# Seven-product pairs whose sums stay in two PSUM banks, in pairs 3 to 21 of the last three feed-forwards

## The chip, the core and the metric

One core of a Trainium2 chip runs the whole program in one launch. TensorE (PE) multiplies, VectorE (DVE), ScalarE (ACT) and GpSimd (POOL) work on tiles, and SyncE (SP) issues most transfers. The metric is the device time of one execution in microseconds (us); lower is better. The median of three runs before the change is 1907.0 us (1905.99 to 1907.22).

## The reference

A decoder trunk of two layers on 512 tokens of 1024 channels, in float32. Each layer has a half-step SwiGLU feed-forward, a token mixer (a causal convolution in layer 0, stick-breaking attention in layer 1) and another half-step feed-forward. So there are four feed-forwards, numbered 0 to 3; the change touches 1, 2 and 3.

```python
def rms_norm(x, g):
    xf = x.astype(jnp.float32)
    y = xf * lax.rsqrt(jnp.mean(xf * xf, axis=-1, keepdims=True) + RMS_EPS)
    return (y * g.astype(jnp.float32)).astype(x.dtype)

def swiglu_ffn(x, w_gate, w_up, w_down):
    return (jax.nn.silu(x @ w_gate) * (x @ w_up)) @ w_down

for layer in range(DEPTH):
    h = h + HALF_STEP * swiglu_ffn(rms_norm(h, ffn1_norm[layer]), ...)
    u = rms_norm(h, mix_norm[layer])
    ...
    h = h + HALF_STEP * swiglu_ffn(rms_norm(h, ffn2_norm[layer]), ...)
```

D_MODEL is 1024 and D_FF 2816, so a feed-forward has 22 hidden blocks of 128.

## The kernel before

Channels lie on the 128 partitions, tokens along the free axis: an activation is eight chunks of 128 x 512. Every number is held as two parts, hi (rounded, matmul type fp32r) and lo (what is left), and each product of blocks is three matmuls: hi x hi, hi x lo, lo x hi (L397 to L399, `mm3`). Weights arrive as raw float32 units of 128 x 1024 (512 KB) on SP's queue and are split in the core: ACT casts raw to whi (L249), DVE subtracts to wlo (L250). `raw`, `whi` and `wlo` have three buffers each.

A feed-forward goes through its 22 hidden blocks in thirds of 8, 8 and 6. For each block f a **pair** is computed: the gate block pg and the up block of 128 x 512 outputs. Then DVE scales by the norm's factor r_f, ACT applies silu, DVE multiplies, and the result is split into hhi and hlo. After each third come eight down products `pd`, each of 8 (or 6) blocks, added into the residual by DVE (L631).

A **plain pair** is two products of 8 chunks x 3 matmuls of 512 columns. A **seven-product pair** (Winograd's form of Strassen's scheme) sees the pair as a 2 x 2 block product: gate and up are two rows, even and odd chunks the inner halves, the two halves of the tokens the columns. Seven products of 4 chunk pairs x 3 matmuls of 256 columns replace eight. They need sums of weights, made for each pair on DVE in `sevens` (st, two changed quarters of raw, their casts sh and uh on ACT, sl and ul on DVE), and sums of inputs, made once per feed-forward on DVE in `right_sums` (xs, ts, then thi on ACT and tlo on DVE; four groups q = 0 to 3 of two chunks each). The products are named by their weight side: "11", "12", "22" are the plain quarters, s1 to s4 the sums. s1 and s2 use the inputs t(0) and t(1), which are the first tile of each q (thi_q_0, tlo_q_0); s3 and "22" use the second.

Which pairs take the form says the table `SEVEN`. In feed-forwards 1 and 3 the first one is pair 5, in 2 it is pair 6, since there DVE and SP also write the inputs of the key and value projection away in pair 0 (`kvt`, 8 rows on DVE, 8 transfers `kvd`). Input sums are made one group in each of the first four pairs. The tiles st and ts share one buffer (STS = 1); sh, sl, uh, ul and the second whi and wlo of a pair have one buffer each. xs, kvt and the norm's diagonals dg_f share two buffers, so the first xs waits for pb_f, the matmuls that read dg_f.

The order of instructions on each engine in the feed-forwards is fixed at build time by a scheduler that simulates the program; each engine then runs its queue in that order.

## Time and profile before

| what | value |
|---|---|
| median of 3 runs | 1907.0 us |
| profiled execution: span | 1904.9 us |
| profiled execution's own time | not listed; the runs lie 1.1 to 2.3 us above the span |
| PE, DVE, ACT, POOL busy | 99%, 69%, 46%, 15% of the span |
| DMA | 237.84 MB, mean 125 GB/s |

A group's line gives source line, engine, operation, tiles, count, then busy time and mean ns of one, then the idle time before them and what ended it. In the timeline a row gives start, duration, engine, line, operation, tiles, and in brackets idle time before it with its releaser. Durations of rows that follow each other directly overlap; the distance of their starts tells what one costs its engine. A wait for several signals is put down to the last.

### The profile page before, as it was taken

To read this page: it belongs to the slowest core of one execution; us is meant where nothing else is said; L and a number is where in the kernel's file an instruction comes from. 1 tells how busy PE (TensorE), PEld (TensorE's weight loads), DVE (VectorE), ACT (ScalarE), POOL (GpSimd) and SP (SyncE) were. 2 spreads that over 40 slices of the span, in tenths; PEclk is the share of its full clock that TensorE was granted. 3 is DMA by queue.
4 is the path that set the end of the run, shared out by engine and by line. 5 is a ranking of instruction groups with operands and counts; after the bars stand their busy time and mean duration, and the time that the engine had idled before them with its cause. 6 is when DMAs were issued, how large, how long until landed. Compare 5 with 4: busy or idle time off the path is not lost.

```text
span 1904.9 us, 26577 instructions
## 1 busy us (share of the span) xinstructions
PE 1884.1 (99%) x10236; PEld 1630.4 (86%) x10236; DVE 1318.5 (69%) x2139; ACT 872.7 (46%) x1385; POOL 288.1 (15%) x267
## 2 busy tenths in 40 slices
PE   9999999999999999999999999999999999999997
PEld 7888888878998889898888988888888788898896
DVE  6544434589869577576775857778989688676575
ACT  5423424586644234244333423446778644343333
POOL 0212302079700000000000000004554100000001
PEclk9999999999999999999999999999999999999998
DMA  5756746444422323333433232442323133332322
GB/s 203 251 180 232 275 146 216 158 172 144 161 78 89 105 89 117 100 94 96 143 111 100 89 111 89 127 155 83 89 70 93 49 123 100 100 95 95 111 86 70
DMA packets 74254, 237.84 MB, mean 125 GB/s; under 512 B 8464, under 2 KB 11152, under 8 KB 74128
## 3 DMA queue, kind: packets, MB, share of 16 engines
q1 hardware_dynamic: 65776, 209.41, 34.0%
q10 hardware_dynamic: 8352, 26.74, 3.8%
q8 instruction: 80, 1.31, 0.3%
q14 instruction: 46, 0.38, 0.1%
HBM read 200.46 MB, written 31.46 MB: 122 GB/s over the span
## 4 chain that ended last, share of the span: by engine, by line
PE 94%; DVE 2%; POOL 1%; ACT 1%; issue 1%; DMA 0%; POOLq 0%; DVEq 0%; ACTq 0%
PE pg L397 11%; PE pg L398 11%; PE pg L399 11%; PE pd L398 8%; PE pd L397 8%; PE pd L399 8%; PE pg L557 6%; PE pg L556 6%; PE pg L555 6%; PE z L1192 2%; PE pa L397 1%; PE pa L398 1%; PE pa L399 1%; PE pv L397 1%; PE pk L397 1%
## 5 line engine op out<-in xcount | busy, mean ns | idle before, releaser
L249 ACT CAST whi<-raw 128x1024 fp32r<-128x1024 f32 (+2 forms) x310 | 313.2, 1013 | 634.6 <-PE pd L398 226.8
L250 DVE TENSOR_TENSOR wlo<-raw,whi 128x1024 fp32r<-128x1024 f32 (+2 forms) x310 | 367.8, 1191 | 43.1 <-ACT whi L249 42.7
L398 PE MATMUL pg<-xlo_f,whi 128*128 128x512 f32 x896 | 349.7, 391 | 0.0
L397 PE MATMUL pg<-xhi_f,whi 128*128 128x512 f32 x896 | 349.0, 391 | 0.6 <-ACT whi L249 0.6
L399 PE MATMUL pg<-xhi_f,wlo 128*128 128x512 f32 x896 | 349.4, 390 | 0.0
L398 PE MATMUL pd<-hlo,whi 128*128 128x512 f32 x686 | 266.2, 389 | 0.0
L399 PE MATMUL pd<-hhi,wlo 128*128 128x512 f32 x686 | 265.1, 389 | 0.0
L397 PE MATMUL pd<-hhi,whi 128*128 128x512 f32 x686 | 264.1, 389 | 0.0
L397 PEld LDWEIGHTS pg<-xhi_f,whi 128*128 128x128 f32 x896 | 169.0, 189 | 35.2 <-ACT whi L249 1.5
L399 PEld LDWEIGHTS pg<-xhi_f,wlo 128*128 128x128 f32 x896 | 168.6, 188 | 34.7 <-DVE wlo L250 0.3
L398 PEld LDWEIGHTS pg<-xlo_f,whi 128*128 128x128 f32 x896 | 168.8, 188 | 33.6
L631 DVE SCALAR_TENSOR_TENSOR xpar<-pd,xpar 128x512 f32<-128x512 f32 x93 | 63.7, 689 | 170.6 <-PE pd L399 170.6
L399 PEld LDWEIGHTS pd<-hhi,wlo 128*128 128x128 f32 x686 | 128.8, 188 | 26.8
L397 PEld LDWEIGHTS pd<-hhi,whi 128*128 128x128 f32 x686 | 128.8, 188 | 26.7
L398 PEld LDWEIGHTS pd<-hlo,whi 128*128 128x128 f32 x686 | 128.8, 188 | 26.6
L1092 POOL TENSOR_SCALAR_AFFINE_SELECT tri<-ones 128x128 f32<-128x128 f32 x1 | 0.6, 592 | 703.7 <-DVE tu L612 703.7
L250 POOL TENSOR_TENSOR plo<-praw,phi 128x1024 fp32r<-128x1024 f32 x24 | 59.0, 2461 | 275.7 <-ACT phi L249 273.9
L875 POOL TENSOR_TENSOR ws<-ws,pr 128x256 f32<-128x256 f32 (+1 forms) x90 | 91.0, 1023 | 58.2 <-ACT pr L873 54.6
L249 ACT CAST hhi<-tu 128x512 fp32r<-128x512 f32 x88 | 54.3, 621 | 87.9 <-DVE tu L586 49.2
L886 DVE SCALAR_TENSOR_TENSOR pc<-gl,xpar,pc 128x512 f32<-128x512 f32 (+1 forms) x145 | 88.3, 646 | 3.9 <-PE pc L865 2.2
L611 DVE TENSOR_TENSOR tu<-pg,r_f 128x512 f32<-128x512 f32 x56 | 38.6, 689 | 74.2 <-PE pg L399 74.2
L556 PE MATMUL pg<-tlo,whi 128*128 128x256 f32 x256 | 72.5, 283 | 0.0
(359 smaller groups left out, 4195.0 us busy)
## 6 DMA issues: line engine op xcount, KB each, us to landing
raw<-in_gu_dram SPq DMA_DIRECT2D x174, 512.0 KB, 3.5
raw<-in_dna_dram SPq DMA_DIRECT2D x64, 512.0 KB, 3.6
praw<-in_pw_dram SPq DMA_DIRECT2D x24, 512.0 KB, 4.4
aparth<-phi ACTq DMA_DIRECT2D x24, 512.0 KB, 2.7
apartl<-plo ACTq DMA_DIRECT2D x24, 512.0 KB, 3.8
raw<-in_dnb_dram SPq DMA_DIRECT2D x32, 384.0 KB, 3.4
whi<-aparth SPq DMA_DIRECT2D x21, 512.0 KB, 3.3
wlo<-apartl SPq DMA_DIRECT2D x21, 512.0 KB, 4.2
```

The source lines that it names most:

```text
L249: ins = A.copy(dst_hi, src)
L250: (G if on_pool else V).tensor_sub(dst_lo, src, dst_hi.bitcast(F32))
L397: PE.matmul(ps, w[0], x[0], start=first, stop=False)
L398: PE.matmul(ps, w[0], x[1], start=False, stop=False)
L399: PE.matmul(ps, w[1], x[0], start=False, stop=last)
L555: PE.matmul(d, a[0], b[0], start=first and q == 0, stop=False, skip_group_check=True)
L556: PE.matmul(d, a[0], b[1], start=False, stop=False, skip_group_check=True)
L557: PE.matmul(d, a[1], b[0], start=False, stop=last_, skip_group_check=True)
L611: V.tensor_mul(tu, pt[1], rb)
L631: V.scalar_tensor_tensor(res[d], pd, 0.5, res[d], op0=ALU.mult, op1=ALU.add)
L875: add("G", 1.28 * f + 0.1 * half, lambda pr=pr: G.tensor_add(accp, accp, pr()[:, at0]), r=[pr], w=[at_], rank=rank)
L886: add("V", 0.66 * f + 0.06 * half, lambda x=x, q=q: V.scalar_tensor_tensor(pc(), x(), q, pc(), op0=ALU.mult, op1=ALU.add), r=[gl], w=[pc], ...
```

## The change

Three things. The table takes in pairs 3 to 21 of feed-forwards 1 to 3. Input sums are made two groups in each of pairs 0 and 1. And a seven-product pair keeps its running sums in two PSUM banks (u0 and g1, opened once per feed-forward by one small matmul each, `seed_banks`): ACT copies a finished sum from bank to bank, PE adds the next product on top, and the DVE additions of the partial sums (m1, v6, v7) go. m5 gets a second buffer.

```diff
-SEVEN = {1: (5, 6, 8, 9, 11, 12, 14, 16, 17, 19, 20), 2: (6, 8, 10, 11, 13, 14, 16, 17, 19, 20), 3: (5, 6, 8, 9, 11, 12, 14, 16, 17, 19, 20)}
+SEVEN = {1: tuple(range(3, 22)), 2: tuple(range(3, 22)), 3: tuple(range(3, 22))}
...
-                product(0, "11", x(0, 0), True)
-                A.copy(m1, at_[0])
-                product(1, "s2", t(1), True)
-                V.tensor_add(v6, at_[1], m1)
-                product(2, "s1", t(0), True)
-                A.copy(m5, at_[2])
-                product(1, "s3", t(2), False)
-                V.tensor_add(v7, at_[1], m1)
-                product(2, "s4", x(1, 1), False)
-                V.tensor_add(tg[:, halves[1]], at_[2], v6)
-                product(0, "12", x(1, 0), False)
-                product(1, "22", t(3), False)
+                product(g0, "11", x(0, 0), True)
+                A.copy(u0, g0)
+                product(m, "s1", t(0), True)
+                A.copy(m5, m)
+                product(u0, "s2", t(1), False)
+                A.copy(g1, u0)
+                product(g0, "12", x(1, 0), False)
+                V.tensor_mul(tg[:, halves[0]], g0, rb[:, halves[0]])
+                product(u0, "s3", t(2), False)
+                V.tensor_add(tu[:, halves[1]], u0, m5)
+                product(g1, "s4", x(1, 1), False)
+                V.tensor_add(tg[:, halves[1]], g1, m5)
                 V.tensor_mul(tg[:, halves[1]], tg[:, halves[1]], rb[:, halves[1]])
-                V.tensor_mul(tg[:, halves[0]], at_[0], rb[:, halves[0]])
                 last[0] = A.activation(tg, tg, AF.Silu)
-                V.tensor_add(tu[:, halves[1]], v7, m5)
-                V.tensor_add(tu[:, halves[0]], at_[1], m1)
-                V.tensor_mul(tu, tu, rb)
+                product(u0, "22", t(3), False)
+                V.tensor_mul(tu[:, halves[1]], tu[:, halves[1]], rb[:, halves[1]])
+                V.tensor_mul(tu[:, halves[0]], u0, rb[:, halves[0]])
+
+            seeds = []
+
+            def seed_banks():
+
+                for j in range(2):
+                    d = ps.tile([P, T], F32, name=f"seed{idx}_{j}", tag="ps", bufs=7)[:, : T // 2]
+                    PE.matmul(d, onesr, norm.x[0][0][:, : T // 2], start=True, stop=True)
+                    seeds.append(d)
...
-                    if f < NC // 2 and idx in SEVEN:
-                        right_sums(f)
+                    if f < 2 and idx in SEVEN:
+                        if not f:
+                            seed_banks()
+                        right_sums(2 * f)
+                        right_sums(2 * f + 1)
```

What it does to the queues, at three places of feed-forward 1. In the names the first number after a tile is the feed-forward's or pair's, the last a buffer's; `seed_0` is u0, `pg_3_1` is m of pair 3.

DVE, where the last input sums are made. Before, the first seven-product pair is 5, and its sl stands ahead of the end of the fourth group, in pair 4:

```order
L250 TENSOR_TENSOR wlo_1_5430<-raw_1_5426,whi_1_5428 128x1024
L609 TENSOR_TENSOR tg_4_5582<-pg_4_0_5501,r_f_0_5108 128x512
L250 TENSOR_TENSOR sl_5440<-st_5433,sh_5439 128x1024
L250 TENSOR_TENSOR wlo_0_5507<-raw_0_5503,whi_0_5505 128x1024
L250 TENSOR_TENSOR ul_5447<-raw_0_5425,uh_5446 128x512
L512 TENSOR_TENSOR ts_3_5488<-xs_6_5484 128x256
L514 TENSOR_TENSOR ts_3_5488<-xs_7_5486,xs_6_5484 128x256
L611 TENSOR_TENSOR tu_4_5583<-pg_4_1_5502,r_f_0_5108 128x512
L513 TENSOR_TENSOR ts_3_5488<-xs_7_5486,ts_3_5488 128x256
L612 TENSOR_TENSOR tu_4_5583<-tu_4_5583,tg_4_5582 128x512
L515 TENSOR_TENSOR ts_3_5488<-xs_7_5486,ts_3_5488 128x256
L250 TENSOR_TENSOR tlo_3_0_5494<-ts_3_5488,thi_3_0_5493 128x512
```

Now the first is pair 3. Behind its sl and ul come the third and fourth group, and between them wlo_0 of pair 5 (raw_0_5412):

```order
L512 TENSOR_TENSOR ts_2_5331<-xs_4_5327 128x256
L514 TENSOR_TENSOR ts_2_5331<-xs_5_5329,xs_4_5327 128x256
L513 TENSOR_TENSOR ts_2_5331<-xs_5_5329,ts_2_5331 128x256
L507 TENSOR_TENSOR xs_6_5344<-xhi_f_0_6_5033,xlo_f_0_6_5034 128x512
L515 TENSOR_TENSOR ts_2_5331<-xs_5_5329,ts_2_5331 128x256
L250 TENSOR_TENSOR tlo_2_0_5337<-ts_2_5331,thi_2_0_5336 128x512
L507 TENSOR_TENSOR xs_7_5346<-xhi_f_0_7_4901,xlo_f_0_7_4902 128x512
L250 TENSOR_TENSOR tlo_2_1_5339<-ts_2_5331,thi_2_1_5338 128x512
L250 TENSOR_TENSOR wlo_0_5416<-raw_0_5412,whi_0_5414 128x1024
L512 TENSOR_TENSOR ts_3_5348<-xs_6_5344 128x256
L514 TENSOR_TENSOR ts_3_5348<-xs_7_5346,xs_6_5344 128x256
L513 TENSOR_TENSOR ts_3_5348<-xs_7_5346,ts_3_5348 128x256
```

So the rest of the fourth group (L515 and tlo_3_0 come next) moved from behind two pairs more of plain work to a place behind all of pair 3's weight sums. In feed-forward 2 the eight kvt rows stand in the same stretch.

PE, the first seven-product pair. Before, in pair 5:

```order
L556 MATMUL pg_5_0_5600<-xlo_f_0_6_5033,whi_0_5427 128x256
L557 MATMUL pg_5_0_5600<-xhi_f_0_6_5033,wlo_0_5429 128x256
L555 MATMUL pg_5_1_5601<-thi_0_0_5207,sh_5439 128x256
L556 MATMUL pg_5_1_5601<-tlo_0_0_5208,sh_5439 128x256
L557 MATMUL pg_5_1_5601<-thi_0_0_5207,sl_5440 128x256
L555 MATMUL pg_5_1_5601<-thi_1_0_5296,sh_5439 128x256
```

Now, in pair 3, with the start of product 11 of pair 4 drawn ahead of it:

```order
L555 MATMUL pg_4_0_5627<-xhi_f_0_6_5033,wlo_0_5367 128x256
L555 MATMUL pg_3_1_5499<-thi_0_0_5211,sl_5283 128x256
L553 MATMUL pg_3_1_5499<-thi_1_0_5228,sh_5282 128x256
L554 MATMUL pg_3_1_5499<-tlo_1_0_5229,sh_5282 128x256
L555 MATMUL pg_3_1_5499<-thi_1_0_5228,sl_5283 128x256
L555 MATMUL seed_0_5198<-thi_0_0_5211,sl_5283 128x256
L553 MATMUL seed_0_5198<-thi_1_0_5228,sh_5282 128x256
L554 MATMUL seed_0_5198<-tlo_1_0_5229,sh_5282 128x256
L555 MATMUL seed_0_5198<-thi_1_0_5228,sl_5283 128x256
L553 MATMUL pg_3_1_5499<-thi_2_0_5336,sh_5282 128x256
L553 MATMUL seed_0_5198<-thi_2_0_5336,sh_5282 128x256
```

Products s1 (into pg_3_1) and s2 (into seed_0) of pair 3 now go side by side, group by group of the input sums, and everything else of pairs 3 and 4 stands behind them.

DVE inside a run. Before, pair 8, in which the sums of pair 9 are made and a plain pair follows:

```order
L250 TENSOR_TENSOR sl_6120<-st_6113,sh_6119 128x1024
L572 TENSOR_TENSOR tg_8_6188<-pg_8_0_6196,r_f_0_5108 128x256
L250 TENSOR_TENSOR wlo_6192<-raw_6190,whi_6191 128x1024
L566 TENSOR_TENSOR v_1_8_6202<-pg_8_1_6197,m_1_8_6199 128x256
L574 TENSOR_TENSOR tu_8_6189<-v_1_8_6202,m_1_8_6200 128x256
L568 TENSOR_TENSOR tg_8_6188<-pg_8_2_6198,v_1_8_6201 128x256
L571 TENSOR_TENSOR tg_8_6188<-tg_8_6188,r_f_0_5108 128x256
L250 TENSOR_TENSOR ul_6127<-raw_0_6105,uh_6126 128x512
L575 TENSOR_TENSOR tu_8_6189<-pg_8_1_6197,m_1_8_6199 128x256
L576 TENSOR_TENSOR tu_8_6189<-tu_8_6189,r_f_0_5108 128x512
L250 TENSOR_TENSOR wlo_1_6110<-raw_1_6106,whi_1_6108 128x1024
```

Now, in pair 10, from ul of pair 11 to the first weight sum of pair 12:

```order
L250 TENSOR_TENSOR ul_6396<-raw_0_6374,uh_6395 128x512
L573 TENSOR_TENSOR tu_10_6631<-seed_0_5198,r_f_0_5108 128x256
L250 TENSOR_TENSOR wlo_1_6379<-raw_1_6375,whi_1_6377 128x1024
L569 TENSOR_TENSOR tg_10_6630<-tg_10_6630,r_f_0_5108 128x256
L592 TENSOR_TENSOR tu_10_6631<-tu_10_6631,tg_10_6630 128x512
L344 TENSOR_TENSOR st_6511<-raw_1_6504 128x4x128
L564 TENSOR_TENSOR tg_11_6759<-pg_11_0_6786,r_f_0_5108 128x256
L345 TENSOR_TENSOR raw_1_6504<-raw_0_6503,raw_1_6504 128x4x128
```

Each pair's sums are now followed at once by the next pair's, whose raw_1 takes the buffer that ul has just let go.

More of the change, by code (lines that the diff above doesn't have):

```diff
@@ L539, in t, with product @@
                     return lambda q: [y[:, halves[j % 2]] for y in right[q][j // 2]]
-                at_ = [
+                g0, m = (
                     ps.tile([P, T], F32, name=f"pg{n}_{j}", tag="ps", bufs=7)[:, : T // 2]
-                    for j in range(3)
-                ]
-                m1, m5, v6, v7 = (
-                    hp.tile([P, T // 2], F32, name=f"{m}_{n}", tag=m, bufs=1)
-                    for m in ("m1", "m5", "v6", "v7")
-                )
-                def product(j, left, rhs, first):
+                    for j in range(2)
+                )
+                u0, g1 = seeds
+                m5 = hp.tile([P, T // 2], F32, name=f"m5_{n}", tag="m5", bufs=2)
+                def product(d, left, rhs, first):
                     for q in range(NC // 2):
-                        a, b, d = w[left](q), rhs(q), at_[j]
+                        a, b = w[left](q), rhs(q)
                         last_ = q == NC // 2 - 1
```

## The prediction

> **What bounds the kernel now.** I read the page first (busy time, the chain that ended last), then the granted clock and busy time by windows, then the timeline of PE and DVE in the feed-forwards that change.
>
> ```profile
> span 1904.9 us, 26577 instructions
> PE 1884.1 (99%) x10236; PEld 1630.4 (86%) x10236; DVE 1318.5 (69%) x2139; ACT 872.7 (46%) x1385; POOL 288.1 (15%) x267
> ...
> PE 94%; DVE 2%; POOL 1%; ACT 1%; issue 1%; DMA 0%; POOLq 0%; DVEq 0%; ACTq 0%
> ...
> 579.00:590.00 11.00, 11.00 (x50) 9.12 (x49) 10.79 (x18) 4.30 (x6) 0.00 (x0) 1.00 0.30 97
> ...
> 706.00:790.00 84.00, 84.00 (x499) 74.96 (x498) 56.30 (x85) 31.47 (x42) 0.00 (x0) 1.00 0.32 101
> ```
>
> PE is busy from end to end, and the chain of waits lies on it for 94%. So any matmul time taken away is gained, as long as PE isn't made to wait instead. The two windows (columns: length, then PE, PEld, DVE, ACT, POOL busy, clock, DMA share, GB/s) are of feed-forward 1. At its start, 579 to 590, DVE has 10.79 of 11 us: it is as full as PE. Over the second third's pairs and part of its down products, 706 to 790, it has 56.30 of 84: there is room only on the average. The page's 69% for DVE hides that.
>
> **What a pair costs PE.** The timeline of PE, first and last of 21 matmuls of a plain pair, then of 36 of a seven-product pair; a row's own 0.40 or 0.28 us overlaps the next, so I take the distance of starts.
>
> ```profile
> 619.71 0.40 PE L397 MATMUL pg<-xhi_f,whi 128*128 128x512 f32 x1
> ...
> 624.27 0.39 PE L399 MATMUL pg<-xhi_f,wlo 128*128 128x512 f32 x1
> ...
> 631.75 0.28 PE L555 MATMUL pg<-xhi_f,whi 128*128 128x256 f32 x1
> ...
> 635.95 0.28 PE L557 MATMUL pg<-xhi_f,wlo 128*128 128x256 f32 x1
> ```
>
> 4.56 us / 20 = 0.228 us for 512 columns, 4.20 / 35 = 0.120 us for 256 (more than half of 0.228). A plain pair has 2 x 8 x 3 = 48 matmuls: 10.94 us. A seven-product pair has 7 x 4 x 3 = 84: 10.08 us. One pair changed over saves 0.86 us, not an eighth. Pairs of the seven-product form go from 11 + 10 + 11 = 32 to 57; 25 x 0.864 = **21.6 us less PE work**. The seed matmuls add 3 x 2 x 0.12 = 0.7 us.
>
> **What a pair costs DVE.** Distances of starts again (L345 to L346; two L250 of 1024; two of 256 columns; two kvt rows as one).
>
> ```profile
> 717.53 0.69 DVE L345 TENSOR_TENSOR raw<-raw,raw 128x512 f32<-128x512 f32 x1
> 718.13 0.69 DVE L346 TENSOR_TENSOR st<-st,raw 128x512 f32<-128x512 f32 x1
> ...
> 719.67 1.22 DVE L250 TENSOR_TENSOR wlo<-raw,whi 128x1024 fp32r<-128x1024 f32 x1
> 720.80 0.69 DVE L350 TENSOR_TENSOR raw<-raw,st 128x512 f32<-128x512 f32 x1
> ...
> 737.17 0.42 DVE L568 TENSOR_TENSOR tg<-pg,v 128x256 f32<-128x256 f32 x1 [0.17 <-PE pg L557]
> 737.51 0.42 DVE L574 TENSOR_TENSOR tu<-v,m 128x256 f32<-128x256 f32 x1
> ...
> 942.30 1.41 DVE L1066 SCALAR_TENSOR_TENSOR kvt<-xpar,r_f 128x512 f32<-128x512 f32 x2
> 943.63 0.68 DVE L250 TENSOR_TENSOR hlo<-tu,hhi 128x512 fp32r<-128x512 f32 x1
> ```
>
> So 512 columns cost 0.60 us, 1024 cost 1.13, 256 cost 0.335, a kvt row 0.665. A seven-product pair had 3 x 1.13 + 5 x 0.60 for its weights, 7 x 0.335 + 0.60 for the sums and scalings, 2 x 0.60 at the end: 10.5 us. The change removes one of 256 and the 512 at L576: 9.6 us. A plain pair costs 2 x 1.13 + 4 x 0.60 = 4.7. So in a run of seven-product pairs DVE has 9.6 us of work for PE's 10.08, where two such pairs and a plain one had 25.7 for 31.1. DVE is no bound by its work alone, but nothing is left over. ACT gains one copy of 256 columns per pair; its row from PSUM to SBUF is below (0.372), from PSUM to PSUM no row shows one; 0 to 0.59 (the 512-column r_f copy) bounds it, and I take 0.37 as the same width. With that, ACT has 2 x 1.05 + 1.05 + 0.62 + 3 x 0.37 + 2 x 0.62, 6.1 us of 10.08: hidden.
>
> ```profile
> L249 ACT CAST whi<-raw 128x1024 fp32r<-128x1024 f32 x266 | 279.6, 1052 | 569.2 <-PE pd L398 198.7 <-PE pg L398 181.8 <-PE pg L556 69.5
> L249 ACT CAST thi<-ts 128x512 fp32r<-128x512 f32 x24 | 14.8, 616 | 8.7 <-DVE ts L513 7.6 <-DVE ts L515 1.0
> L560 ACT COPY m<-pg x32: 362/372/376, 610.8 to 1839.8; 128x256 f32<-128x256 f32 x32
> L422 ACT COPY r_f<-pb_f x4: 587/589/589, 43.4 to 1556.0; 128x512 f32<-128x512 f32 x4
> raw<-in_gu_dram SPq DMA_DIRECT2D x174, 512.0 KB, 3.5
> kvd<-kvt SPq DMA_DIRECT2D x8, 256.0 KB, 2.6
> ```
>
> **The starts.** The first seven-product pair moves from pair 5 or 6 to pair 3, so all input sums and that pair's weight sums have to be done two or three plain pairs (22 to 33 us) sooner, and DVE makes them. Its queue from the first xs to tlo_3_0, on which PE's s1 and s2 products of pair 3 wait, holds 32 instructions of 512 columns, 17 of 256 and 6 of 1024: 19.2 + 5.7 + 6.8 = 31.7 us; in feed-forward 2 also 8 kvt: 37.0. The first xs can't come sooner: it waits for pb_f on PE, whose place doesn't move.
>
> ```profile
> 570.77 0.69 DVE L507 TENSOR_TENSOR xs<-xhi_f,xlo_f 128x512 f32<-128x512 f32 x1 [3.36 <-PE pb_f L419]
> 587.60 0.69 DVE L611 TENSOR_TENSOR tu<-pg,r_f 128x512 f32<-128x512 f32 x1 [0.16 <-PE pg L399]
> ...
> 923.10 0.69 DVE L507 TENSOR_TENSOR xs<-xhi_f,xlo_f 128x512 f32<-128x512 f32 x1 [3.46 <-PE pb_f L419]
> 961.45 0.69 DVE L611 TENSOR_TENSOR tu<-pg,r_f 128x512 f32<-128x512 f32 x1 [0.58 <-PE pg L399]
> ...
> 1555.05 0.69 DVE L507 TENSOR_TENSOR xs<-xhi_f,xlo_f 128x512 f32<-128x512 f32 x1 [3.46 <-PE pb_f L419]
> 1571.65 0.69 DVE L611 TENSOR_TENSOR tu<-pg,r_f 128x512 f32<-128x512 f32 x1 [0.17 <-PE pg L399]
> ```
>
> The L611 rows tell when PE had finished pair 2 (587.60, 1571.65; in feed-forward 2 the row shown is pair 4's, less 2 x 10.94: 939.6). After that PE has 54 matmuls of 256 columns (11 and 12 of pair 3, 11 of pair 4, three quarters of s1 and s2) before it needs tlo_3_0: 6.5 us. Feed-forward 1: needed at 594.1, there at 570.77 + 31.7 = 602.5, **8.4 us late**. Feed-forward 2: 946.1 against 960.1, **14.0**. Feed-forward 3: 1578.2 against 1586.8, **8.6**. Sum 31.0. PE's queue has nothing else before these products, so it stands still.
>
> That takes DVE as never idle. It will be: tg of pair 3 stands in its queue behind PE's product 12, which waits for the PSUM copy after 11 (about 1 us in 1 and 3); and wlo_0 of pair 5 comes before the last sums. Its raw tile takes a buffer of pair 3, and SP issues it behind the load that waits for ul of pair 3: 0.7 for two issues + 3.5 + 1.05 for the cast, against 3.8 us of DVE work between, so 1.4 us; in feed-forward 2 also an xs behind the kvd transfer (2.6 us), together 3.3. With signals and the thi cast (0.62) behind the last L513, 0.5 each: 2.9 + 3.8 + 2.8 = 9.5 us (bounds 0 and 16). From the middle I take 9.5.
>
> **Inside the runs.** The second raw tile of pair n+1 takes the buffer that ul of pair n frees. From ul to ul: issue 0.35, load 3.5, then DVE's queue from L344 to the next ul, 6 x 0.60 + 4 x 0.335 + 2 x 1.13 = 7.2: 11.05 us for PE's 10.08, 1.0 us lost per pair once the lead is used up. The lead comes from the down products: after s2 of a pair PE has five products (7.2 us) before the next pair's s1 needs sl, and sl takes a cast of 1.05 and 1.13 on DVE, so at most 5.0 us can be in hand. Pairs 8 to 15, seven steps, then lose 2; 16 to 21, five steps, none; 3 to 7, four steps that start with little in hand, 1: 3 us each feed-forward, 9 in all (bounds 0, and 57 pairs x 1.0). I take 9, since two of three runs start behind down products.
>
> The two seeds hold two of seven PSUM banks; down products then have five, each needs one for 5.46 us of PE and 0.60 of DVE: hidden.
>
> **The sum.** 1904.9 - 21.6 + 0.7 + 31.0 + 9.5 + 9 = 1933.5. The page doesn't show the profiled execution's own time beside its span; the median of the runs, 1907.0, lies 2.1 above, and with that it is **1935.6 us**, say 1935.
>
> **What a standing PE does to its clock.** The windows at the end of the program and two equal pairs of matmuls:
>
> ```profile
> 1893.00:1894.00 1.00, 0.10 (x1) 0.01 (x1) 0.93 (x4) 0.18 (x1) 1.00 (x3) 1.00 0.69 236
> 1894.00:1895.00 1.00, 0.00 (x0) 0.00 (x0) 0.97 (x2) 0.00 (x0) 1.00 (x2) 0.54 0.69 238
> 1895.00:1896.00 1.00, 0.00 (x0) 0.00 (x0) 0.93 (x3) 0.36 (x1) 0.91 (x2) 0.50 0.88 297
> ...
> 1891.04 0.40 PE L1351 MATMUL pb_out0v<-dg_out,onesr 128*128 128x256 f32 x2
> ...
> 1898.04 0.82 PE L1351 MATMUL pb_out1v<-dg_out,onesr 128*128 128x256 f32 x2 [4.93 <-ACT dg_out L1342]
> ```
>
> PE's last work ended at 1893.1, the granted clock was half by 1894.1, and the same pair took 0.82 for 0.40. No row shows how long it takes to come back. The stands at the starts are of 3 to 9 us, so they can do this. [...]
>
> **The rivals.** (a) The clock: if it stays half after a stand for as long as the longest gap lasted (5, 9, 5 us), half of that is lost again: + 9.5, 1945. For it the rows just shown; against it that DVE, not PE, holds the pace of the next pairs, so part is hidden. (b) The starts are shorter: DVE packed without a gap and the runs without loss: 1935 - 18.5 = 1917. (c) No lead: each of the 57 pairs loses 1.0: 1935 - 9 + 55 = 1981; against it the 56.30 of 84 us above. (d) Other side: DVE's start work turns out to be hidden, because PE needs the sums later than I count. Decided where the three stands together are under 21.6 - 9 = 12.6 us; with none it is 1907 - 21.6 + 9, about 1895. Against it: even without the 3.4 us of DVE idleness ahead of each first xs, 31.0 would only fall to 21. (e) The two cancel: 1907.
>
> **How the numbers follow.** Forecast 0.41, (a) 0.23, (b) 0.16, (c) 0.07, (d) 0.09, (e) 0.04. The range takes in the forecast, (a) and (b): 1915 to 1952. About 0.2% (4 us) is what a measurement tells from no change: faster 0.09, within 0.04, slower 0.87. That is some 1.5% more time than before.
>
> **What would show it.** In the profile after: matmuls of 256 columns at 0.120 us and 57 x 84 of them; PE idle ahead of the first L553 to L555 rows of pair 3 in each of the three feed-forwards, ended by DVE's sl or tlo, 11 us or so in 1 and 3 and some 18 in 2; DVE without gaps there; a dip of the granted clock behind them if (a) holds; waits of DVE's L344 for raw's transfer inside the runs. If PE is not idle at those places, the step on the starts is wrong, and with it the sign.

## The result, and the profile after

The changed kernel takes 1985.5 us (median of four runs, 1981.25 to 1987.09) for 1907.1 before (four runs): a ratio of 1.0408, 95% interval 1.0393 to 1.0423. It is 78.4 us slower. The forecast of 1935 had the sign and about a third of the size, and the time lies far outside the range of 1915 to 1952. The profiled execution took 1984.1 with a span of 1982.4.

From the page after: span, busy times, shares of the chain that ended last, and groups of matmuls (count, busy time, mean ns, idle time before them and its releaser).

```profile
span 1982.4 us, 28659 instructions
PE 1905.3 (96%) x11142; PEld 1676.9 (85%) x11142; DVE 1411.6 (71%) x2325; ACT 947.3 (48%) x1542; POOL 287.7 (15%) x267
...
PE 82%; DVE 8%; ACT 4%; DMA 3%; POOL 2%; issue 1%; POOLq 0%; ACTq 0%; DVEq 0%
...
L397 PE MATMUL pd<-hhi,whi 128*128 128x512 f32 x686 | 266.9, 396 | 8.7 <-ACT hhi L249 5.8
...
L553 PE MATMUL pg<-xhi_f,whi 128*128 128x256 f32 x456 | 130.9, 287 | 1.3 <-ACT seed L558 1.3
```

Two more groups, from the list of PE's groups:

```profile
L553 PE MATMUL seed<-thi,sh 128*128 128x256 f32 x228 | 68.3, 300 | 12.2 <-ACT seed L558 11.6
L553 PE MATMUL pg<-thi,sh 128*128 128x256 f32 x228 | 68.3, 300 | 29.6 <-ACT thi L249 18.1 <-ACT sh L249 11.3
```

PE's share of the chain fell from 94% to 82%. 456 is 57 pairs x 8, so the form stands in all 57. The waits for thi and sh (29.6 us) lie nearly all at the three starts. The waits for u0 (tile `seed`, copy at L558) come back pair after pair, and the down products wait for hhi.

The table gives the time of each third, from the last matmul of the norm's row pb_f (first third) or of the down products before, to the last down product, by PE's timeline in each profile. e3 to e13 are experiments below.

| third | before | after | e3 | e7 | e10 | e13 | e11 |
|---|---|---|---|---|---|---|---|
| FF1, first | 112.3 | 125.9 | 114.1 | 125.8 | 126.5 | 121.9 | 112.5 |
| FF1, second | 126.7 | 130.4 | 130.0 | 131.0 | 129.2 | 126.0 | 126.0 |
| FF1, last | 94.8 | 99.5 | 98.4 | 96.6 | 96.8 | 94.3 | 94.3 |
| FF2, first | 112.9 | 134.6 | 115.1 | 134.5 | 133.4 | 131.9 | 113.3 |
| FF2, second | 126.7 | 130.2 | 130.3 | 130.7 | 128.9 | 126.3 | 126.9 |
| FF2, last | 94.8 | 100.1 | 100.0 | 96.5 | 98.7 | 95.0 | 95.0 |
| FF3, first | 112.1 | 127.9 | 113.9 | 125.1 | 125.1 | 121.9 | 112.5 |
| FF3, second | 126.7 | 131.5 | 130.1 | 130.5 | 130.0 | 126.0 | 126.2 |
| FF3, last | 82.6 | 87.5 | 87.8 | 83.6 | 85.8 | 82.3 | 82.3 |

The nine thirds take 78.0 us more, so the loss lies in them: 51.1 in the first thirds, 26.9 in the six later ones. With the 0.864 us that each of 25 added pairs saves, the losses are 59.7 and 39.9. The forecast had 43.5 and 6.

The rows of PE tell more closely where the time went. Take the distance from each matmul's start to the next one's, less the pace of 0.120 us for 256 columns and 0.228 for 512, and add it up by place: at the starts (the first 50 us behind pb_f), in the pairs behind them, and at the down products. Before loses 0.4 us in all, after 98.0.

| us that PE loses | forecast | after | e2 | e3 | e6 | e7 | e9 | e10 |
|---|---|---|---|---|---|---|---|---|
| at the starts | 40.5 | 52.5 | 53.9 | 0.0 | 47.5 | 52.2 | 51.2 | 46.2 |
| in the pairs behind | 9 | 25.9 | 37.8 | 23.5 | 27.1 | 25.6 | 63.3 | 8.0 |
| at the down products | 0 | 19.6 | 13.4 | 19.1 | 15.7 | 0.1 | 18.1 | 29.9 |

Of the 52.5 us at after's starts, 16.2 are matmuls that follow one another at half clock. With the first line drawn at 70 us, some 2 us of after and e10 move from the second row to the first.

The start of feed-forward 1 in PE's timeline and DVE's (start, duration, engine, line, tiles; in brackets idle time before the row). The last DVE row is of feed-forward 2.

```profile
587.88 0.28 PE L555 MATMUL pg<-xhi_f,wlo 128*128 128x256 f32 x1
588.61 0.38 PE L553 MATMUL pg<-xhi_f,whi 128*128 128x256 f32 x1 [0.45 <-ACT seed L558]
...
593.49 0.58 PE L553 MATMUL pg<-thi,sh 128*128 128x256 f32 x1 [3.18 <-ACT sh L249]
...
599.65 0.28 PE L555 MATMUL seed<-thi,sl 128*128 128x256 f32 x1
603.96 0.58 PE L553 MATMUL pg<-thi,sh 128*128 128x256 f32 x1 [4.03 <-ACT thi L249]
```

```profile
569.72 0.69 DVE L507 TENSOR_TENSOR xs<-xhi_f,xlo_f 128x512 f32<-128x512 f32 x1 [3.40 <-PE pb_f L419]
...
590.34 0.42 DVE L564 TENSOR_TENSOR tg<-pg,r_f 128x256 f32<-128x256 f32 x1 [1.03 <-PE pg L555]
...
601.02 1.23 DVE L250 TENSOR_TENSOR wlo<-raw,whi 128x1024 fp32r<-128x1024 f32 x1 [1.23 <-ACT whi L249]
...
603.94 1.29 DVE L250 TENSOR_TENSOR tlo<-ts,thi 128x512 fp32r<-128x512 f32 x2 [0.23 <-ACT thi L249]
```

```profile
978.56 0.69 DVE L507 TENSOR_TENSOR xs<-xhi_f,xlo_f 128x512 f32<-128x512 f32 x1 [5.01 <-DMA kvd<-kvt]
```

PE stands where it was forecast, ended by sh and then by the last thi (the forecast named sl and tlo, which DVE makes from these two casts). On DVE the two small gaps that were named (tg behind PE's 12, wlo of pair 5 behind its late load) are there with 1.03 and 1.23 us. In feed-forward 2 the wait for kvd is 5.01 instead of some 2.6. From the first xs to the end of tlo_3_0 DVE took 34.8, 43.2 and 34.7 us, by the starts of the rows; the forecast's terms give 34.6, 40.8 and 34.5.

Windows of the same stretch (length, then PE, PEld, DVE, ACT, POOL busy, granted clock, DMA share, GB/s):

```profile
589.20:592.60 3.40, 1.10 (x10) 0.90 (x8) 2.37 (x6) 1.32 (x3) 0.00 (x0) 0.99 0.02 5
592.60:599.40 6.80, 5.92 (x27) 5.92 (x28) 6.80 (x12) 2.59 (x4) 0.00 (x0) 0.50 0.46 154
599.40:602.80 3.40, 0.53 (x5) 0.32 (x3) 2.17 (x4) 1.04 (x1) 0.00 (x0) 1.00 0.00 1
602.80:609.60 6.80, 5.20 (x21) 4.68 (x22) 6.00 (x11) 2.92 (x5) 0.00 (x0) 0.50 0.00 0
```

After each of these two stands the clock is half for 6.8 us, and 256 columns then cost 0.213 us for 0.120. In the whole trace, ten such stretches of 61 us in all lie ahead of the program's end, where before there was none.

### The profile page after: what moved, and what is told of

Same layout as the page of the kernel before. It is cut to its first block, busy times and chain, and to the rows that moved or that the text cites. A ratio compares the mean times of both kernels' runs of the same rounds, so it can differ in the third digit from the quotient of the medians.

```text
span 1982.4 us, 28659 instructions
## 1 busy us (share of the span) xinstructions
PE 1905.3 (96%) x11142; PEld 1676.9 (85%) x11142; DVE 1411.6 (71%) x2325; ACT 947.3 (48%) x1542; POOL 287.7 (15%) x267
## 4 chain that ended last, share of the span: by engine, by line
PE 82%; DVE 8%; ACT 4%; DMA 3%; POOL 2%; issue 1%; POOLq 0%; ACTq 0%; DVEq 0%
PE pd L397 8%; PE pd L399 8%; PE pd L398 8%; PE pg L399 6%; PE pg L397 6%; PE pg L398 5%; PE seed L553 5%; PE seed L554 4%; PE seed L555 4%; PE pg L553 3%; PE pg L555 3%; PE pg L554 3%; DMA raw<-in_gu_dram 2%; DVE wlo L250 2%; PE z L1201 2%; ACT whi L249 1%
## 5 line engine op out<-in xcount | busy, mean ns | idle before, releaser
L250 DVE TENSOR_TENSOR wlo<-raw,whi 128x1024 fp32r<-128x1024 f32 (+2 forms) x310 | 367.5, 1191 | 45.9 <-ACT whi L249 45.1
L399 PE MATMUL pg<-xhi_f,wlo 128*128 128x512 f32 x496 | 193.3, 390 | 0.6 <-DVE wlo L250 0.5
L398 PE MATMUL pg<-xlo_f,whi 128*128 128x512 f32 x496 | 193.0, 389 | 0.0
L397 PE MATMUL pg<-xhi_f,whi 128*128 128x512 f32 x496 | 192.1, 390 | 0.2 <-ACT whi L249 0.2
L397 PEld LDWEIGHTS pd<-hhi,whi 128*128 128x128 f32 x686 | 129.6, 189 | 42.3 <-ACT whi L249 10.7
L398 PEld LDWEIGHTS pd<-hlo,whi 128*128 128x128 f32 x686 | 130.2, 190 | 26.3 <-DVE hlo L250 0.4
L553 PE MATMUL seed<-thi,whi 128*128 128x256 f32 x456 | 131.7, 289 | 2.7 <-ACT seed L562 2.7
L553 PE MATMUL pg<-xhi_f,whi 128*128 128x256 f32 x456 | 130.9, 287 | 1.3 <-ACT seed L558 1.3
L555 PE MATMUL pg<-xhi_f,wlo 128*128 128x256 f32 x456 | 130.7, 287 | 0.0
L554 PE MATMUL pg<-xlo_f,whi 128*128 128x256 f32 x456 | 130.6, 286 | 0.0
L554 PE MATMUL seed<-tlo,whi 128*128 128x256 f32 x456 | 130.6, 286 | 0.0
L555 PE MATMUL seed<-thi,wlo 128*128 128x256 f32 x456 | 130.6, 286 | 0.0
L399 PEld LDWEIGHTS pg<-xhi_f,wlo 128*128 128x128 f32 x496 | 93.1, 188 | 20.9 <-DVE wlo L250 1.3
L397 PEld LDWEIGHTS pg<-xhi_f,whi 128*128 128x128 f32 x496 | 93.1, 188 | 20.2 <-ACT whi L249 1.1
```

Source lines behind the costliest of these rows:

```text
L250: (G if on_pool else V).tensor_sub(dst_lo, src, dst_hi.bitcast(F32))
L397: PE.matmul(ps, w[0], x[0], start=first, stop=False)
L398: PE.matmul(ps, w[0], x[1], start=False, stop=False)
L399: PE.matmul(ps, w[1], x[0], start=False, stop=last)
L553: PE.matmul(d, a[0], b[0], start=first and q == 0, stop=False, skip_group_check=True)
L554: PE.matmul(d, a[0], b[1], start=False, stop=False, skip_group_check=True)
```

## The experiments

The kernel before was run beside them again: its medians are 1906.6 to 1907.0. The first four ask for the form, the table, the starts and the clock.

**e1 and e5, the form alone.** After's pair form with before's table and one input group in each of pairs 0 to 3:

```diff
-SEVEN = {1: tuple(range(3, 22)), ...}
+SEVEN = {1: (5, 6, 8, 9, 11, 12, 14, 16, 17, 19, 20), ...}
-                    if f < 2 and idx in SEVEN:
+                    if f < NC // 2 and idx in SEVEN:
                         if not f:
                             seed_banks()
-                        right_sums(2 * f)
-                        right_sums(2 * f + 1)
+                        right_sums(f)
```

> The new form of the pair alone: the table of the kernel before (11, 10 and 11 pairs) and its input sums, one group in each of pairs 0 to 3. Theory (the starts and the dense runs carry the loss): PE gets 0.7 us more work for the seeds, and the waits of PE for the copies from bank to bank, which in the changed kernel add up to about 3 us in the middle third of eight dense pairs, stay small with plain pairs between: 1907 to 1912. Rival (the form itself costs): each of 32 pairs waits for its copies as the first pair of a third does, 0.6 + 1.45 us, so 1907 + 0.7 + 66 = 1973.

Measured 1990.6 us (ratio 1.0439, 1.0423 to 1.0454): neither. All nine thirds were within 1.8 us of before; the stretch with the attention took 376.7 us for 297.5. ScalarE's timeline at the end of feed-forward 2, and its groups in the attention:

```profile
1224.97 1.28 ACT L1262 ACT_TABLE_LOAD   x1
...
1226.90 1.28 ACT L570 ACT_TABLE_LOAD   x1
1228.77 0.63 ACT L570 ACTIVATE tg<-tg 128x512 f32<-128x512 f32 x1 [0.59 <-DVE tg L569]
```

```profile
L1210 ACT ACT_TABLE_LOAD x46 | 59.0, 1283 | 0.8
...
L1241 ACT ACT_TABLE_LOAD x26 | 33.4, 1283 | 0.5
...
L1209 ACT ACT_TABLE_LOAD x21 | 26.9, 1283 | 0.4
```

The load of the table that serves the attention's exp and ln together is tied to the silu that stands last in the text. The scheduler put the silu of pair 20 (L570) behind it, so the silu table came back, and from there each exp and ln loaded its own: 99 loads for 5. e5 ties the load to the last three silus:

```diff
-            with tc.issue_after(last[0].ins):
+            with tc.issue_after(silus[-1].ins), tc.issue_after(silus[-2].ins), tc.issue_after(silus[-3].ins):
                 table = A.preload_act_table_set("natural_log_exp_and_others")
```

> The new form with the old table again, as in the first run of it (1990.6), with one thing more: the load of ScalarE's function table for the attention is tied to the last three silus of feed-forward 2, not to the one that is last in the program's text. In that first run the feed-forwards were within 1 to 4 us of the kernel before, and the attention took 376.7 us for 297.5, with 99 loads of a function table of 1.28 us each for 5. Theory (the loads took the 79 us, the form itself costs little): 5 loads, attention 297 to 299, 1908 to 1914. Rival (the form costs something in the attention by other means, such as tile placement): the attention stays near 376, about 1990.

Measured 1911.9 (ratio 1.0025, 1.0015 to 1.0034), 5 loads, 297.3 us in the attention: with the 94 loads, 120.6 us of ScalarE's time, the 79 us are gone. (The load is tied in this way in e7, e11, e13 and e14 too.) The form itself costs 4.8 us over 32 pairs. After's own trace has 5 loads, so this is no part of its loss.

**e2, the table alone.** Before's pair form with after's table and input sums.

> The pair as it was before (sums kept in SBUF by DVE), with the new table (pairs 3 to 21) and the input sums in pairs 0 and 1. Theory (DVE's work at the starts and in the runs carries the loss): DVE has 10.5 us per pair for PE's 10.08, 0.42 us lost in most of 57 pairs, so 15 to 25 us over the changed kernel's 1985.5: about 2005. Rival (the copies from bank to bank carry much of the loss in the thirds, some 3 us per third): without them the kernel comes below the changed one, about 1960 to 1975.

Measured 1988.7 (1.0431, 1.0415 to 1.0446), between the two. Waits for u0 are gone, since the old form has none, but in the second third of feed-forward 1 PE waits for sh in five pairs running, the first, second and third of them here:

```profile
730.24 0.39 PE L555 MATMUL pg<-thi,sh 128*128 128x256 f32 x1 [0.90 <-ACT sh L249]
...
742.29 0.39 PE L555 MATMUL pg<-thi,sh 128*128 128x256 f32 x1 [1.72 <-ACT sh L249]
...
753.46 0.39 PE L555 MATMUL pg<-thi,sh 128*128 128x256 f32 x1 [0.83 <-ACT sh L249]
```

That is the loss of about 1.0 per dense pair of rival (c), in the old form. In the new one other waits take its place, for about the same total: PE loses 25.9 us in the pairs for e2's 37.8, but 19.6 at the down products for 13.4.

**e3, a later start.** `SEVEN = tuple(range(6, 22))` in all three, input sums one group in each of pairs 0 to 3.

> The changed kernel with the first seven-product pair at 6 instead of 3 (pairs 6 to 21), and the input sums one group in each of pairs 0 to 3, as before. PE work: 48 seven-product pairs, 16 more than before, 16 x 0.864 = 13.8 us less, 0.7 more. Theory (each start costs its own stand, the later thirds their own 6 to 7 us): the stands at the three starts (59.8 us lost in the first thirds of the changed kernel) fall to about 3 in all, the losses in the second and last thirds (39.6) stay: 1907.1 - 13.1 + 42.6 = 1937. Rival (DVE is behind from the start on and drags the backlog through the thirds): the later losses shrink too, to 10 or so, about 1905.

Measured 1935.4 (1.0152, 1.0137 to 1.0167): the first theory to 2 us. The first thirds fall back to 1.8 to 2.2 us over before; the later thirds are 2.6 us shorter than after's in all. Starts and later thirds are separate costs, and hardly any backlog is carried from the one to the other.

**e4, matmuls in the stands.** They go to a bank of their own and wait for what is there already. Product 12 of pair 3 moves ahead of s1 in the text, where PE's queue had it anyway. One of the two places (the other is between the groups of s1):

```diff
+                    with tc.issue_after(end.ins):          # end: last matmul of product 12 of pair 3
+                        for _ in range(FILL[idx][0]):
+                            PE.matmul(spare, onesr, norm.x[0][0][:, : T // 2], start=True, stop=True)
```

> The changed kernel with matmuls that nothing reads, put where PE stands in pair 3: about 3.1 and 6 us of them in feed-forwards 1 and 3, 4.3, 10 and 1.7 us in 2, ahead of the products that wait for the input sums. They make no input ready sooner; PE only does not stand. Theory (the half clock behind the stands costs time): the granted clock stays at 1.00 there, and the products behind the last stand of each start, which lose 2.5, 2.8 and 2.5 us at half clock, run at 0.120 us: about 1985.5 - 8 = 1977.5. Rival (the half clock hides under DVE's pace): 1985 to 1988. Other rival (all that was run at half clock, 5.2 + 5.3 + 5.3 us, comes back): 1969.5.

Measured 1979.2 (1.0381, 1.0364 to 1.0398), 6.3 us less than after; the expected 8 was near. The intervals of the two just touch, so the size is rough. The two windows of e4 that had a clock of 0.50 in after (same columns):

```profile
592.60:599.40 6.80, 5.60 (x44) 5.17 (x43) 6.80 (x12) 3.11 (x5) 0.00 (x0) 1.00 0.46 151
...
602.80:609.60 6.80, 6.25 (x50) 5.84 (x49) 6.40 (x14) 2.84 (x5) 0.00 (x0) 1.00 0.01 2
```

The clock is full in both. In after, the matmuls inside half-clock stretches came 22 us behind their pace in all; only 6.3 came back. The expectation had counted what lies behind the last stand of each start (7.8), since ahead of it PE waits for DVE anyway.

The next four ask what costs time inside the runs.

**e6, two banks for u0.** `u0, g1 = seeds[f % 2], seeds[2]`, three seeds.

> The changed kernel with two banks for u0, used in turn by odd and even pairs, so that the copy of the next pair's first product need not wait for this pair's last readers. The waits of PE for that copy are 1.45 + 0.23 + 0.82 us in the middle third of feed-forward 1, 1.45 + 0.23 in the last third, some 0.6 to 1.4 in the first, with refills of 0.1 to 0.26 behind each. Theory (these waits are a cost of their own): they go, 4 to 5 us per feed-forward, about 1985.5 - 13 = 1972. Rival (the loop of ul, the load and L344 sets the pace under them): PE waits for sh or sl instead, 1982 to 1988.

Measured 1975.7 (1.0361, 1.0347 to 1.0375): 9.8 less. The time is nearer the theory's 1972 than the rival's, but not for the theory's reason. The waits for u0 ahead of s2 (11.6 us in after) are gone, and others have come, these two groups among them (in after 2.7 and 1.3):

```profile
L553 PE MATMUL seed<-thi,whi 128*128 128x256 f32 x456 | 133.6, 293 | 7.5 <-ACT seed L562 4.0 <-DVE tu L566 3.0
L553 PE MATMUL pg<-xhi_f,whi 128*128 128x256 f32 x456 | 130.7, 287 | 4.8 <-ACT seed L558 4.8
```

In the pairs PE loses 27.1 us for 25.9, no less than before. The gain lies at the starts (5.0, where 6.5 us less are lost at half clock; the granted clock is 0.988 in the mean for after's 0.982), at the down products (3.9) and in the attention (1.9), whose code is the same. Why it lies there is open.

**e7, plain pairs 7, 15 and 21.**

> The changed kernel with the last pair of each third plain (7, 15 and 21), as in the kernel before: 9 seven-product pairs less, 9 x 0.864 = 7.8 us more PE work (table load tied as in the run above). Theory (a seven-product pair at a third's end makes the down products wait: whi 1.0 with refills 0.2 behind pairs 7 and 15, hhi 1.9 and 1.5 of half clock behind pair 21): 3 x (1.2 + 1.2 + 3.4) = 17.4 us less, 1985.5 + 7.8 - 17.4 = 1976. Rival (the plain pair also gives DVE and the loads their lead back, so the waits within the next run shrink too): 1965 to 1970. Other rival (the waits move one pair forward and stay): 1993.

Measured 1970.6 (1.0333, 1.0319 to 1.0347), 14.9 less with 7.8 more PE work. The time is at the first rival's upper end, but the mechanism is the theory's: the down products lose 0.1 us for 19.6 (17.4 were expected), and the pairs lose 25.6 for 25.9, where the rival had them lose less.

```profile
L397 PE MATMUL pd<-hhi,whi 128*128 128x512 f32 x686 | 265.0, 389 | 0.0
```

By the thirds, with the 0.864 added back, the last thirds gain 3.8, 4.5 and 4.8, the second ones 0.3, 0.4 and 1.9, the first 1.0, 1.0 and 3.7. So pair 21 matters most.

**e8, before with three pairs more.** Before's form; 5, 6, 8, 9, 10, 12, 13, 14, 16, 17, 18, 20 (feed-forward 2 without 5).

> The kernel before, its own pair form and input sums, with one seven-product pair more in each feed-forward, placed in runs of three with a plain pair between: 5, 6, 8, 9, 10, 12, 13, 14, 16, 17, 18, 20 (feed-forward 2 without 5). Theory (PE loses only where runs are longer than what the lead covers; three in a row are covered): 3 x 0.864 = 2.6 us less, 1904.3. Rival (each dense pair loses 1.0 as soon as two stand before it): 10 pairs or so x 1.0 more, 1912 to 1914.

Measured 1909.0 (1.0012, 1.0003 to 1.0021): the 2.6 us don't come, and neither does the rival's loss. The three pairs more are in the second thirds, and PE waits once in each, 0.9 us beyond its pace, for a copy m that ACT makes late:

```profile
740.97 0.39 PE L555 MATMUL pg<-xhi_f,uh 128*128 128x256 f32 x1 [0.74 <-ACT m L564]
```

That takes back what the pair saved. In feed-forward 1 smaller waits for sums, 0.2 to 0.35, come behind it.

**e9, e10: raw free early.** a12 - s2 goes to its own tile:

```diff
-        V.tensor_sub(a12, a12, s2)
+        u4 = p.tile([P, NC // 2, P], F32, name=f"u4{i}", tag="u4", bufs=1)
+        V.tensor_sub(u4, a12, s2)
-        split(uh, ul, a12)
+        split(uh, ul, u4)
```

> The changed kernel with one step of the weight sums written to a tile of its own (2 KB per partition) instead of back into raw (L350, a12 - s2): raw's buffer comes free after that DVE step and no longer after uh and ul, which come about 3.9 us later, so the second load of the next pair can start that much sooner and the loop ul, load, L344, ul falls from some 11.0 us to 7. Theory (that loop sets the pace of the dense runs): the waits for sl, and behind DVE those for the copies into u0, shrink in all nine thirds by about 2 us each: 1985.5 - 18 = 1967. Rival (the single bank u0 and DVE's own work set the pace; the load was late without effect): 1982 to 1987.

Measured 2018.4 (1.0588, 1.0572 to 1.0604), 33 us more: outside both. The scheduler chose another order (presumably because the weights come sooner): it put the last four matmuls of product 11 straight ahead of s2, and s2 adds onto the copy of what 11 leaves:

```profile
739.10 0.28 PE L556 MATMUL pg<-xhi_f,wlo 128*128 128x256 f32 x1
740.24 0.39 PE L554 MATMUL seed<-thi,sh 128*128 128x256 f32 x1 [0.86 <-ACT seed L559]
```

1.14 us from start to start where 0.120 is the pace: 1.02 us in nearly every pair. ACT's rows at the same place:

```profile
738.86 1.05 ACT L249 CAST whi<-raw 128x1024 fp32r<-128x1024 f32 x1 [0.46 <-ACT tg L571]
739.82 0.37 ACT L559 COPY seed<-pg 128x256 f32<-128x256 f32 x1
```

Product 11 was done at 739.38, and DVE had read the bank by 739.37; the copy stands behind a cast of whi in ACT's queue until 739.82. With ACT free, the way from a product over its copy to the next one takes 0.73 from start to start, 0.61 beyond the pace (587.88 to 588.61 in after's rows above). So about 0.4 of the 1.02 us are the cast's. With the second bank (e10) the wait is gone:

> The two edits of the runs before together: raw free early, and two banks for u0 in turn. Two banks alone gave 9.8 us of the 13 expected. Theory (loop and bank are two separate costs): the gains add, about 10 + 18 us, 1957; what stays is the starts (about 50 us over the kernel before) and the ends of the thirds. Rival (they hide one another): the better one of the two alone, 1967 to 1975.

Measured 1971.1 (1.0343, 1.0328 to 1.0357): 14.4 less than after, 47 less than e9 and 4.6 less than e6 (the intervals of these two overlap). In time it is as the rival said, and PE's rows tell how. In the pairs PE loses 8.0 us, 17.9 less than in after. But at the down products it loses 29.9, 10.3 more: it waits at each third's end for the last block, presumably because it comes there sooner (16.4 us idle for 8.7 in after's row above):

```profile
L398 PE MATMUL pd<-hhi,whi 128*128 128x512 f32 x686 | 266.7, 397 | 16.4 <-ACT hhi L249 14.0 <-ACT whi L249 2.2
```

**e12, lo parts on GpSimd.** `split(..., on_pool=True)` for tlo and the seven-product pairs' hlo.

> The changed kernel with the subtractions for tlo (8 of 512 columns per feed-forward) and for hlo of the seven-product pairs on GpSimd, whose rows of 512 columns take 1.30 us for DVE's 0.60, and which is idle there. Theory (DVE's queue from the first xs to the last input sum sets the starts): DVE has 4.8 us less at each start and 0.6 less in each pair, the last sum comes 0.7 later behind DVE's last step: about 4 us less at each start and 1 to 2 in each third, 1985.5 - 20 = 1965. Rival (st and ts share a buffer, so each group now waits for 2.6 us of GpSimd's work instead of 1.2 of DVE's): starts no shorter or up to 4 us longer, 1980 to 1995.

Measured 2002.5 (1.0504, 1.0489 to 1.0518), slower than the rival. GpSimd's groups, and DVE's first weight sum in e12 and after:

```profile
L250 POOL TENSOR_TENSOR hlo<-tu,hhi 128x512 fp32r<-128x512 f32 x57 | 83.5, 1466 | 828.9 <-ACT hhi L249 774.2 <-issue 23.6 <-PE seed L555 20.2
...
L250 POOL TENSOR_TENSOR tlo<-ts,thi 128x512 fp32r<-128x512 f32 x24 | 40.5, 1706 | 211.9 <-ACT thi L249 161.8 <-DMA raw<-in_gu_dram 50.1
```

```profile
L344 DVE TENSOR_TENSOR st<-raw 128x512 f32<-128x512 f32 x57 | 56.7, 995 | 39.2 <-DMA raw<-in_gu_dram 27.7 <-POOL tlo L250 11.4
```

```profile
L344 DVE TENSOR_TENSOR st<-raw 128x512 f32<-128x512 f32 x57 | 39.3, 690 | 16.4 <-DMA raw<-in_gu_dram 15.8
```

GpSimd's rows are 1.47 and 1.71 us in the mean where those of the convolution are 1.30 (L875 of before). DVE's L344 is 0.995 for after's 0.690 and L345 behind it 1.053 for 0.685, while the weight sums that follow, L346 and L350, are 0.701 and 0.681 for 0.685 and 0.686. L344 also waits for tlo, because st and ts share a buffer. From the first xs to the end of tlo_3_0 it became longer (36.3 for 34.8 us in feed-forward 1). Most of the loss lies behind the starts, though: PE loses 41.1 us in the pairs for 25.9, and waits there 25 times for tu, 17.0 us.

**e13, all that helped,** in one kernel: e4, e7 and e10.

> The changed kernel, first seven-product pair still 3, with all four edits that helped one by one: matmuls that nothing reads in the stands of pair 3 (6.3 us gained alone), two banks for u0 and raw free early (14.4 together), plain pairs 7, 15 and 21 (14.9 alone, with 7.8 of PE work paid). Theory (four separate costs): 1985.5 - 35.6 = 1950. Rival (what is left then is the starts alone): PE work of 48 pairs for 32, 1907 - 13.8 + 0.9, plus the stands of some 40 us, 1934. Other rival (the plain ends and the quicker loop gave the same microseconds twice): 1956 to 1962.

Measured 1940.4 (1.0178, 1.0162 to 1.0194): 45.1 less than after, more than the 35.6 that the single gains add up to, and between the theory and the first rival. The second and last thirds are from 0.7 below before to 0.2 above (nine pairs more of the new form should have saved 7.8 us there, so 5.4 are still lost); of PE's waits by cause (engine, line, releaser: us in total, times, longest) only the first is over 2.1 us, and it lies at the program's end:

```profile
PE pb_out1v L1377 <- ACT dg_out L1368: 4.9, 1, 4.9
PE pg L561 <- ACT sh L250: 2.1, 4, 0.8
PE pg L561 <- ACT seed L567: 1.8, 4, 0.4
```

What stays is mainly the starts: the first thirds are 9.6, 19.0 and 9.8 over before, and with 2, 3 and 2 pairs more in them (0.864 each) the starts cost 11.3, 21.6 and 11.5.

**e11 and e14, towards a faster kernel.** e10's pair; input sums in pairs 0 to 3; pairs 5, 6, 8 to 14, 16 to 20 (e14: 5 to 20; feed-forward 2 without 5 in both).

> The two edits of the run before, with input sums one group in each of pairs 0 to 3 as in the kernel before, and pairs 5, 6, 8 to 14, 16 to 20 (feed-forward 2 without 5), that is 41 seven-product pairs: no early start and plain pairs at the ends of the thirds. Against the kernel before, 9 pairs more, 9 x 0.864 = 7.8 us less PE work, 0.9 us more for seeds, and some 0.4 us per third of refills, as the new form with the old table showed (4.8 us in all). Theory (starts and ends of thirds cost most, and the runs are cured): 1907 - 7.8 + 4.8 + 2 = 1906. Rival (runs of seven and five dense pairs still lose 3 to 4 us each): 1907 - 3 + 20 = 1924.

Measured 1903.6 (0.9987, 0.9978 to 0.9995). It is 3.1 us below the kernel before and 2.4 below the theory. Of 6.9 us less PE work the thirds kept 0.6: PE loses 5.2 us in the pairs, 2.9 of it in waits for whi. Of the rest, 1.1 lies in the attention and 1.0 ahead of feed-forward 1, where there are no pairs of this form. These two stretches differ by up to 2.2 and 1.1 us among 15 of the 16 profiles (e1's attention left out), so that part can't be put down to the change.

> The late table of the eleventh run (1903.6) with pairs 7, 11 to 15 and 19 filled up as far as they were not: pairs 5 to 20 of feed-forwards 1 and 3, 6 to 20 of 2, 47 seven-product pairs for 41. PE work: 6 x 0.864 = 5.2 us less. Theory (a seven-product pair at the end of a third costs about 1.2 us of down products that wait for whi, as in the changed kernel): 1903.6 - 5.2 + 6 x 1.2 = 1905.6. Rival (with raw free early those waits are gone too): 1898.5.

Measured 1914.2 (1.0041, 1.0028 to 1.0054), 10.7 more than e11: worse than both. e14 adds only pairs 7 and 15 to e11. Pair 15, at the end of the second third, is the cause that shows: that third takes 130.0, 128.9 and 128.9 us for 126.0, 126.9 and 126.2. Its first down products wait for the last block:

```profile
781.54 0.67 PE L398 MATMUL pd<-hhi,whi 128*128 128x512 f32 x1 [1.89 <-ACT hhi L249]
```

The granted clock of e14's profile is 0.995 in the mean for 0.997 before.

## Why the prediction was right in sign and wrong in size

**PE work: right.** 0.120 us per 256 columns and 57 pairs; nothing in the traces speaks against 21.6.

**The starts: right.** DVE's queue from the first xs to tlo_3_0 holds the 32, 17 and 6 rows that were counted, and in feed-forward 1 PE had 54 matmuls of 256 columns ahead of the last wait, as counted. Forecast with all waits: 11.3, 17.8 and 11.4, in all 40.5. e13, where nearly all else is gone, has 11.3, 21.6 and 11.5, in all 44.4. The 3.8 us too few are feed-forward 2's: DVE's queue there takes 42.3 us in e13 for the 40.8 of the forecast's terms, and 2.3 us are lost in the pairs behind that start. e3 shows the other way round that without the early start they go. So the mechanism and its order of causes held.

**The clock: a rival, and true.** The sum left it out; the rival had 9.5 and e4 measured 6.3. The half-clock stretches of after begin and end 3.41 us or a multiple apart (592.56 to 599.38 and 602.80 to 609.62 in feed-forward 1). The rival had 5, 9 and 5 us of half clock at the three starts, and after has 13.7, 20.5 and 13.7, most of it hidden behind DVE's pace. A wait of 1.73 us inside a third (pair 21's hhi, at 902.0) was followed by 3.4 us of half clock as well.

**Inside the runs: the step that failed.** It took 9 us for the pairs and nothing for the down products behind them. PE's rows give 25.9 and 19.6; with the 52.5 at the starts that is 98.0 of the 99.3 us lost (78.4, and 20.9 of PE work saved). Three parts of the step were wrong.

First, the copies into u0 were costed by ACT's busy time, "hidden" in 6.1 of 10.08 us. What counts is PE's way from one product over the copy to the next, and the copy's place in ACT's queue: 0.61 us with ACT free, 1.02 behind a cast of whi (e9), and 1.45 behind the first pair of the later thirds in after. There (712.21) DVE had read the bank by 711.38, but the cast of whi, 710.84 to 711.88, held the copy until 711.79. Waits for u0 ahead of s2 come to 12.2 of the 25.9 us, waits for the copy into g1 to 1.8.

Second, the ends of the thirds weren't costed. Pairs 7, 15 and 21 had been plain, and the down products behind them were covered by that. As seven-product pairs they leave their block late; after's PE behind pair 21 of feed-forward 1:

```profile
902.00 0.96 PE L397 MATMUL pd<-hhi,whi 128*128 128x512 f32 x3 [1.73 <-ACT hhi L249]
...
904.24 0.63 PE L398 MATMUL pd<-hlo,whi 128*128 128x512 f32 x1
904.67 0.63 PE L399 MATMUL pd<-hhi,wlo 128*128 128x512 f32 x1
```

A wait, and then a half clock at which 512 columns cost 0.43 us for 0.228. In e7 plain ends gave 14.9 us net of 7.8 us more PE work, so they were worth 22.7, of which 19.5 show at the down products. The prediction had pairs 16 to 21 lose none.

Third, the loop of ul, load and L344, and the lead of 5.0 us from the down products. In the old form (e2) the lead lasted for two pairs: in the second third of feed-forward 1 PE waits for sh from pair 11 on. In the new form the loop hardly shows by itself, waits for sl and sh are 3.7 of the 25.9 us. From ul to ul it is 9.2 to 13.0 us in after's middle third of feed-forward 1, 11.0 in the mean, for 11.05 forecast, but that is also what a pair takes with all its waits, so it doesn't tell what sets the pace. A second bank alone (e6) and raw free early alone (e9) took nothing off the pairs' loss; both together (e10) took 17.9. That points to two limits side by side, of which the forecast had one. (The 1 us for pairs 3 to 7, "with little in hand", doesn't follow from the forecast's own terms either: four steps at 1.0 are up to 4.)

Rival (c) gave 1981, close to the result, and that is luck: it had 55 us in the pairs by one mechanism of 1.0 each, where the rows have 25.9, and nothing for the down products or the clock. All four remedies together gave 52.9 (45.1 and the 7.8 paid) for 43.4 added one by one. The 9.5 between are close to the 10.3 us that e10 lost more at the down products than after, which plain ends take away. Rival (b) is out by the trace, (d) by PE's stands at the starts, (e) by the time.

## What to carry to other kernels

A cover is a resource: before taking away the plain work at the edges of a stage, cost what then starts bare, here the first down products and the copy from bank to bank, by the path from engine to engine and by what stands ahead in the copying engine's queue, not by its busy time. Look at a remedy by place and not only by its total: e6 and e7 each came near one story's time for another reason. Two remedies can hide one another or, as with raw free early, turn against you alone because the scheduler picks another order, so run them together as well. And look outside the changed stage: an order hung on "the last instruction in the text" moved a function table's load and cost 79 us where nothing had been edited.

## What the hardware showed beside that

In after's trace the eleven stretches at half clock begin whole multiples of 3.41333 us after one another, to 3 ns. Of the ten ahead of the program's end four last 3.41 us, five 6.83 and one 13.65. The length of a wait doesn't tell by itself whether such a stretch follows. At the end of the attention PE waited for 0.73 and then for 1.32 us in after as in before. In after half clock began at 1568.77, in before none followed: the first windows behind it (1514.0 to 1524.2) have a clock of 1.00. The second wait and the row behind it, in after and in before:

```profile
1568.16 0.73 PE L397 MATMUL po<-oh,whi 128*128 128x512 f32 x2 [1.32 <-ACT oh L249]
1568.89 0.80 PE L398 MATMUL po<-ol,whi 128*128 128x512 f32 x1
```

```profile
1516.82 0.73 PE L397 MATMUL po<-oh,whi 128*128 128x512 f32 x2 [1.32 <-ACT oh L249]
1517.54 0.50 PE L398 MATMUL po<-ol,whi 128*128 128x512 f32 x1
```

The way back is clearer. The ten stretches are 18 lengths of 3.41 us. The 8 in which PE was busy for 2.71 us or less were each followed by another one at half clock, the 10 in which it was busy for 2.97 or more by full clock.

In e1 a function table's load took ScalarE 1.283 us (the mean of L1210's 46). The next instruction began 1.30 us after the start of the one at L1262 (1224.97 to 1226.27), and no further gap shows there.

Some of VectorE's rows were longer with one of GpSimd beside them. In after the 250 rows of wlo (L250, 128 x 1024) with no GpSimd row beside them took 1.22 us in the mean, the 14 that shared 40% or more of their time with one 1.56. In e12 GpSimd's hlo took from 1.28 to 2.32 us and DVE's L344 0.995 in the mean for after's 0.690. In the convolution that doesn't show: GpSimd's rows (L875 of before, 512 columns) took 1.29 to 1.34 with DVE busy beside them for 98% of their time, and DVE's (L895 of after, 512 columns) stayed at 0.751 in the mean, 87 of the 88 with one of GpSimd beside them for 40% or more of their time.
